# One diffusion layer on one Trainium2 core: the third and fourth part of the first modulation from split float32r operands

## The chip, the cores and the metric

One NeuronCore of a Trainium2 chip runs the whole kernel in one launch. The metric is the device time in microseconds (us), median of several executions; lower is better. Inputs and outputs are float32.

## What is computed

One layer of a latent diffusion backbone: 1024 latent tokens and 256 context tokens of 1024 features, with two SwiGLU feed-forward blocks (inner width 2816) around a mixing block of attention and a short convolution. What matters here is the modulation. A vector `c` (and `c_ctx` for the context tokens) gives nine rows of 1024 numbers, of which rows 0 and 1 shift and scale the input of the first feed-forward block:

```python
m  = (silu(c)     @ w_ada + b_ada).reshape(b, 1, 9, d)
mc = (silu(c_ctx) @ w_ada + b_ada).reshape(1, 1, 9, d)
x   = x   + 0.5 * m[:, :, 2]  * swiglu(rmsnorm(x, g)   * (1 + m[:, :, 1])  + m[:, :, 0],  w_in, w_out)
ctx = ctx + 0.5 * mc[:, :, 2] * swiglu(rmsnorm(ctx, g) * (1 + mc[:, :, 1]) + mc[:, :, 0], w_in, w_out)
```

The mixing block and the second feed-forward block follow in the same manner, and a final RMSNorm.

## The kernel before, in words

Features lie on the 128 partitions, in eight chunks (`KD` = 8, index d or k), tokens along the free dimension. The latent tokens are two blocks of 512, `L0` and `L1`; the context tokens are one block of 256, `CX`. Matrix products with float32 operands are done as three float32r matmuls: an operand is split into a high part (a ScalarE cast to float32r) and a low part (the float32 value less the high part, rounded to float32r), and high times high, high times low and low times high are added in PSUM.

**Modulation rows 0 and 1.** `ada01(e, chs)` computes them in four parts, e = 0 to 3. Part e covers features 256e to 256e + 255 of both rows, which are the norm chunks d = 2e and 2e + 1. Its weights are two tiles of 128 x 4 x 512 floats (1 MB each), loaded by `load_ch`. It is a float32 matmul (L113) with the two columns of `cs` (silu of `c` and of `c_ctx`) as the stationary operand and 512 columns of weights moving, for eight k; each float32 matmul stands in the trace as two passes. ScalarE copies the result to SBUF (`mrow`, L116), PE transposes it in four pieces (`pc`, L121), and DVE adds the bias into `mod` (L124) and forms the scale `amod` (L127).

**Norm chunks.** `norm_chunk(b, which, d)` multiplies x by `amod` and by the reciprocal norm on DVE (L246), adds the shift and casts to the high part on ScalarE (L248), and makes the low part on DVE (L249). For CX the product goes to a temporary `nt`; for L0 and L1 it stays in place.

**The head** (`head`, L760 to L861) is the order around the change. It loads x of L0, the weights of parts 0 and 1 and the first units of the feed-forward weights, forms the L0 norm, and computes parts 0 and 1. Then it loads the weights of part 2 (two tiles of the tag `hh`), x of CX and L1, and the weights of part 3 (in the tile `A2`). The first two feed-forward units of L0 are then done by k: `pf(d)` is a block of twelve matmuls (four units, three products) for chunk d, into four PSUM banks of the tag `in`. Between these blocks stand, in the order of the program:

- after `pf(1)`: the square sum of CX and its norm into the temporary `rcx`, the square sum of L1 (its norm goes into the temporary `rl1`), and `cx_norm` of chunks 0 to 3;
- before `pf(3)`: part e = 2; after it, its `mrow`, transposes and `mod`, the L0 chunks 4 and 5, the rest of the L1 norm, L1 chunks 0 to 3, and CX chunks 4 and 5;
- before `pf(5)`: part e = 3; after it, the same with L0 chunks 6 and 7 and CX chunks 6 and 7;
- then the gated products of L0 (`sg`), the rest of L1's chunks, the two context units (L292 to L294, PSUM tags `o` and `in`), and `conv_by_k` for L1 (L402 to L404), beside which DVE makes the sums and differences of `tsum_steps` (`t1f` and the T tiles). Phase A (L508 to L510) follows.

L1's high and low parts of chunks 4 to 7 share the tile `A2` with the weights of part 3.

**What sets the order.** The program is written in one order; a scheduler that runs while the kernel is built orders each engine's instructions by the order of the program and by when they become ready by its own estimate. Each engine then works through its list in that order. Temporaries come from pools: `t2` is one tag with six buffers of 128 x 512 floats, for the squares `sq` and sums `ssum`, `rcx`, `rl1`, `nt`, `mrow`, `sg`, `t1f`, the sums `s1`, `s2`, `s4` of a unit's weights (L485 to L487) and more. A tile waits until a buffer of its tag is free. In PSUM the tag `in` has four banks, `o` three and `m` one; `pm` and `pc` of `ada01` and the sums of CX use `o`.

```python
def t2(name, shape=None, dt=F32):
    return tp.tile(shape or [P, 512], dt, tag="t2", name=name, bufs=6)
```

In the head all loads are issued by SP. GpSimd (POOL) first appears with `s1`, `s2`, `s4` of unit 2 (L485 to L487, piece "S" of `prep`, called in `head` beside step 5 of `conv_by_k`, behind piece "gA", which casts `wgA`).

Of the kernel before, what the change touches and what calls it, by code (L numbers as in the profile page):

```python
# [6 lines left out]
F32 = mybir.dt.float32  # L7
F32R = mybir.dt.float32r
AF = mybir.ActivationFunctionType
ALU = mybir.AluOpType  # L10
AX = mybir.AxisListType

P = 128
D = 1024
KD = D // P
# [12 lines left out]
def layer_kernel(  # L28
# [18 lines left out]
    pe, act, dve, sp = nc.tensor, nc.scalar, nc.vector, nc.sync  # L47

    base = ctx.enter_context(tc.tile_pool(name="base", bufs=1))
# [3 lines left out]
    def slot(tag, shape, dt, name):  # L53
        return base.tile(shape, dt, tag=tag, name=name)

    def t2(name, shape=None, dt=F32):
        return tp.tile(shape or [P, 512], dt, tag="t2", name=name, bufs=6)
# [4 lines left out]
    cst = base.tile([P, 148], F32, name="cst")  # L62
    sp.dma_start(cst, const_d)
    ident = cst[:, 0:128]
# [12 lines left out]
    cs = base.tile([P, 2, 8], F32, name="cs")  # L77
    mod = base.tile([P, 2, 9, 8], F32, name="mod")
    amod = base.tile([P, 2, 3, 8], F32, name="amod")

    def col(nm, i=0, n=1):
        return vec[:, OFF[nm] + i:OFF[nm] + i + n]
# [7 lines left out]
    def ps(tag, shape, name):  # L90
        return psum.tile(shape, F32, tag=tag, name=name, bufs=psbufs[tag])
# [8 lines left out]
    def finish_mod(j, ms):  # L100
        for m in ms:
# [5 lines left out]
            if m in (2, 8):  # L107
                dve.tensor_scalar(mod[:, j, m, :], mod[:, j, m, :], 0.5, None, op0=ALU.mult)

    def ada01(e, chs):  # L110
        pm = ps(PTAG, [2, 512], "pm01")
        for k in range(KD):
            pe.matmul(pm, cs[:, :, k], chs[k // 4][:, k % 4, :], start=(k == 0), stop=(k == KD - 1))  # L113
        yield
        mrow = t2("mrow", [2, 512])
        act.copy(mrow, pm)  # L116
        yield
        pc = ps("o", [P, 2, 2, 2], "pc")
        for m in range(2):
            for i in range(2):  # L120
                pe.transpose(pc[:, m, i, :], mrow[:, m * 256 + i * P:m * 256 + (i + 1) * P], ident[0:2, 0:2])  # L121
        bias = col("b", 0, 16).rearrange("p (m d) -> p m d", m=2)
        for j in range(2):
            dve.tensor_tensor(mod[:, j, 0:2, 2 * e:2 * e + 2], pc[:, :, :, j], bias[:, :, 2 * e:2 * e + 2], op=ALU.add)  # L124
        for i in range(2):
            d = 2 * e + i
            dve.tensor_scalar(amod[:, :, 0, d], mod[:, :, 1, d], 1.0, col("nf1", d), op0=ALU.add, op1=ALU.mult)  # L127
# [58 lines left out]
    def load_x(b, src, t0):  # L186
        v = src.rearrange("(d p) t -> p d t", p=P)
        for h in range(2):
            sp.dma_start(b.x[h], v[:, 4 * h:4 * h + 4, t0:t0 + b.N])
# [36 lines left out]
    def split_h(b, dt_name):  # L226
        hi = slot(b.htags[0], [P, KD, b.N], F32R, f"h{b.name}h")
        lo = slot(b.htags[1], [P, KD, b.N], F32R, f"h{b.name}l")
        return hi, lo

    def norm_stat_steps(b, r=None, tag="m", e=dve):
        N = b.N
        s = t2("ssum", [P, N])
        act.activation(s, xd(b, 0), AF.Square)
        for d in range(1, KD):
            q = t2("sq", [P, N])
            act.activation(q, xd(b, d), AF.Square)
            e.tensor_tensor(s, s, q, op=ALU.add)
            if d % 2 == 1:
                yield  # L240
        b.r = rstd_bcast(s, N, D, b.name, tag, r)

    def norm_chunk(b, which, d, keep=True):
        hi, lo = b.h
        t = t2("nt", [P, b.N]) if keep else xd(b, d)
        dve.scalar_tensor_tensor(t, xd(b, d), amod[:, b.j, which, d:d + 1], b.r, op0=ALU.mult, op1=ALU.mult)  # L246
        bias = mod[:, b.j, (0, 3, 6)[which], d:d + 1]
        act.activation(hi[:, d, :], t, AF.Identity, bias=bias)  # L248
        dve.scalar_tensor_tensor(lo[:, d, :], t, bias, hi[:, d, :].bitcast(F32), op0=ALU.add, op1=ALU.subtract)  # L249
# [16 lines left out]
    pool = nc.gpsimd  # L266
# [35 lines left out]
    def adv(gen, n=1):  # L302
        for _ in range(n):
            if next(gen, "end") == "end":
                return False
        return True
# [447 lines left out]
    def x_slots(b):  # L754
        b.x = [slot(t, [P, 4, b.N], F32, f"x_{b.name}") for t in b.xtags]

    PTAG = "o"
    F1 = FFN(1, wi1_d, wo1_d, 2, 0, "01c", "A3", "A2")

    def head():  # L760
        L0.h = split_h(L0, "h")
        units = [(ff, n) for ff in range(2) for n in ("g", "u")]
        ch = {}

        def load_ch(e, tags):
            if len(tags) == 1:
                t = slot(tags[0], [P, 2, 4, 512], F32, "ach")
                ch[e] = [t[:, 0], t[:, 1]]
            else:
                ch[e] = [tp.tile([P, 4, 512], F32, tag=t, name="ach", bufs=2) for t in tags]  # L770
            for i in range(2):
                sp.dma_start(ch[e][i].rearrange("p k c -> p (k c)"), ada01_d[2 * e + i])

        load_x(L0, xt_d, 0)
        load_ch(0, ("A2",))
        F1.load_one(*units[0])
        load_ch(1, ("A3",))
        warm = ps("in", [P, 128], "warm")
        for _ in range(30):
            pe.matmul(warm, ident, ident, start=True, stop=True)  # L780
        for _ in norm_stat_steps(L0):
            pass
        for e in range(2):
            a01 = ada01(e, ch[e])
            next(a01)
            if e == 1:
                for d in range(2):
                    norm_chunk(L0, 0, d, False)
                for u in units[1:]:
                    F1.load_one(*u)  # L790
            next(a01)
            next(a01, None)
        load_ch(2, ("hh", "hh"))
        load_x(CX, ctxt_d, 0)
        x_slots(L1)
        load_x(L1, xt_d, 512)
        load_ch(3, ("A2",))
        CX.h = split_h(CX, "h")
        pt = {u: ps("in", [P, 512], "pf") for u in units}
        hi, lo = L0.h  # L800
        for d in range(2, 4):
            norm_chunk(L0, 0, d, False)

        def pf(d):
            for u in units:
                w = F1.w[u[0]][u[1]]
                wh = w[:, 0, d * P:(d + 1) * P]
                wl = w[:, 1, d * P:(d + 1) * P]
                pe.matmul(pt[u], wh, hi[:, d, :], start=(d == 0), stop=False)
                pe.matmul(pt[u], wl, hi[:, d, :], start=False, stop=False)  # L810
                pe.matmul(pt[u], wh, lo[:, d, :], start=False, stop=(d == KD - 1))

        def l1_norm(ds):
            for d in ds:
                norm_chunk(L1, 0, d, False)

        def cx_norm(ds):
            for d in ds:
                norm_chunk(CX, 0, d)

        F1.split_l1()
        for d in range(KD):
            if d in (3, 5):
                e = (d + 1) // 2
                a01 = ada01(e, ch[e])
                next(a01)
            pf(d)
            if d == 1:
                for _ in norm_stat_steps(CX, t2("rcx", [P, 256]), "o"):
                    pass  # L830
                s1 = norm_stat_steps(L1, t2("rl1"))
                adv(s1, 4)
                cx_norm(range(0, 4))
            if d in (3, 5):
                next(a01)
                next(a01, None)
                norm_chunk(L0, 0, 2 * e, False)
                norm_chunk(L0, 0, 2 * e + 1, False)
            if d == 3:
                adv(s1, 9)  # L840
                l1_norm(range(0, 4))
                cx_norm(range(4, 6))
            if d == 5:
                cx_norm(range(6, KD))
        for ff in range(2):
            F1.gated(ff, L0, pt[(ff, "g")], pt[(ff, "u")])
        l1_norm(range(4, 6))
        F1.conv(0, CX, "o")
        l1_norm(range(6, KD))
        F1.conv(1, CX, "in")  # L850
        F1.load(2)
        ts = F1.tsum_steps()
        for i, _ in enumerate(F1.conv_by_k((0, 1), L1)):
            adv(ts)
            if i == 5:
                F1.prep(2, "gA")
                F1.prep(2, "S")
        for piece in ("sA", "sB", "uA"):
            F1.prep(2, piece)
        run(ts)  # L860
        F1.load(3)  # L861

    def run(g):
        for _ in g:
            pass
# [12 lines left out]
    def last_a(F):  # L878
# [6 lines left out]
        return last  # L885

    head()
    F1.phase_b_init()
    F1.phase_a(2, side_a, {2: ("gA",), 3: ("S",), 4: ("sA",), 7: ("uA",), 8: ("sB",)}, last_a(F1))
# [945 lines left out]
```

## Time and profile before

| | |
|---|---|
| runs of the kernel before | 2165.2, 2167.05 and 2167.07 us; median 2167.05 |
| the profiled execution | 2168.2 us, of which its trace spans 2166.4 |
| TensorE (PE) matmuls | 2130.6 us busy, 98% of the span, 10084 instructions |
| PE weight loads (PEld) | 1711.8 us, 79% |
| VectorE (DVE) | 1546.3 us, 71% |
| ScalarE (ACT) | 910.1 us, 42% |
| GpSimd (POOL) | 227.6 us, 11%, 158 instructions |
| granted clock of PE | 0.995 of full speed, as a mean |

The trace is of one execution. A busy time is a sum over instructions; matmuls are pipelined, so a busy PE is not a PE at its peak. The share over the whole span says little of the head, which is the first 108 us; a change there is read from its own stretch. A granted clock of 1.00 is 2.4 GHz, one of 0.50 is 1.2 GHz.

### The profile page before, as it was taken

What the parts mean: (1) busy time and instruction counts of PE and PEld (TensorE: products, weight loads), DVE (VectorE), ACT (ScalarE), POOL (GpSimd) and SP (SyncE); (2) the same over time, 40 slices, a digit from 0 to 9 for tenths busy, and PEclk for the clock granted to TensorE, in tenths of its full rate; (3) what the DMA queues carried; (4) which work ended last, traced back from release to release, by engine and by line L of the source; (5) the groups of instructions that cost most, each with busy time, mean ns of one, the idle gap of its engine ahead of it and who ended that gap; (6) DMA issues with size and microseconds to landing.
All of it is one profiled execution on the core that took longest, in us unless ns stands there. A gap on an engine that the chain in (4) does not pass through costs nothing.

```text
span 2166.4 us, 26536 instructions
## 1 busy us (share of the span) xinstructions
PE 2130.6 (98%) x10084; PEld 1711.8 (79%) x10084; DVE 1546.3 (71%) x2109; ACT 910.1 (42%) x1415; POOL 227.6 (11%) x158
## 2 busy tenths in 40 slices
PE   8999999999999999999999999999999999999998
PEld 4788788888889887887777777777788888877877
DVE  5887776666657867661898899876866666668754
ACT  4422322222335533442567777754422232234433
POOL 0001111101010110000100100001011111123001
PEclk9999999999999999999999999999999999999998
DMA  8043344545379756342211101142232322378642
GB/s 323 16 146 127 124 147 138 167 130 170 127 242 341 263 178 228 119 136 68 88 49 30 40 20 68 49 151 73 78 99 101 117 94 91 107 287 283 225 147 78
DMA packets 111824, 296.01 MB, mean 137 GB/s; under 512 B 10704, under 2 KB 17872, under 8 KB 108624
## 3 DMA queue, kind: packets, MB, share of 16 engines
q1 hardware_dynamic: 111696, 294.32, 40.1%
q8 instruction: 79, 1.29, 0.2%
q14 instruction: 49, 0.40, 0.1%
HBM read 235.29 MB, written 56.36 MB: 135 GB/s over the span
## 4 chain that ended last, share of the span: by engine, by line
PE 75%; DVE 6%; DMA 4%; issue 2%; ACT 2%; POOL 0%; DVEq 0%; SPq 0%; ACTq 0%; POOLq 0%
PE p L508 9%; PE p L510 9%; PE p L509 9%; PE po L704 6%; PE po L706 6%; PE po L705 6%; DMA wa<-in_ada_dram 3%; PE pT L1331 1%; PE pT L1330 1%; PE pmo L1110 1%; PE pmo L1111 1%; PE pmo L1112 1%; PE pvo L1354 1%; PE pvo L1355 1%; PE pvo L1353 1%
## 5 line engine op out<-in xcount | busy, mean ns | idle before, releaser
L704 PE MATMUL po<-gst,wo 128*128 128x512 f32 (+1 forms) x636 | 248.4, 391 | 3.4 <-DVE x L667 3.4
L706 PE MATMUL po<-gst,wo 128*128 128x512 f32 (+1 forms) x636 | 247.2, 389 | 4.0 <-DVE wo L310 4.0
L705 PE MATMUL po<-gst,wo 128*128 128x512 f32 (+1 forms) x636 | 247.3, 389 | 0.0
L309 ACT CAST gst<-grt 128x1024 fp32r<-128x1024 f32 (+1 forms) x95 | 88.9, 936 | 218.7 <-PE po L706 96.4
L310 DVE TENSOR_TENSOR gst<-grt,gst 128x1024 fp32r<-128x1024 f32 (+1 forms) x95 | 110.6, 1165 | 73.7 <-ACT gst L309 73.5
L706 PEld LDWEIGHTS po<-gst,wo 128*128 128x128 f32 x636 | 120.0, 189 | 31.9 <-DVE wo L310 5.1
L704 PEld LDWEIGHTS po<-gst,wo 128*128 128x128 f32 x636 | 120.1, 189 | 31.5 <-issue 2.7
L705 PEld LDWEIGHTS po<-gst,wo 128*128 128x128 f32 x636 | 120.2, 189 | 26.4
L142 DVE SCALAR_TENSOR_TENSOR acc<-wa,cs,acc 128x1024 f32<-128x1024 f32 x70 | 90.5, 1314 | 60.3 <-DMA wa<-in_ada_dram 60.3
L508 PE MATMUL p<-h0h,wgA 128*128 128x512 f32 x320 | 126.6, 396 | 0.2 <-ACT e1f L528 0.2
L509 PE MATMUL p<-h0l,wgA 128*128 128x512 f32 x320 | 126.4, 395 | 0.0
L510 PE MATMUL p<-h0h,wgA 128*128 128x512 f32 x320 | 126.4, 395 | 0.0
L1333 ACT ACTIVATE pexp<-pT 128x512 f32<-128x512 f32 x160 | 94.5, 598 | 66.6 <-PE pT L1331 35.1
L309 ACT CAST wsB<-s 128x512 fp32r<-128x512 f32 x80 | 48.5, 620 | 152.9 <-DVE s L495 83.0
L277 DVE TENSOR_TENSOR wm<-wr,wm 128x1024 fp32r<-128x1024 f32 x52 | 64.8, 1249 | 42.3 <-ACT wm L273 42.0
L310 DVE TENSOR_TENSOR wo<-wr,wo 128x1024 fp32r<-128x1024 f32 x72 | 83.3, 1163 | 15.2 <-ACT wo L309 15.2
L310 DVE TENSOR_TENSOR wsA<-s,wsA 128x512 fp32r<-128x512 f32 x80 | 51.8, 687 | 54.3 <-ACT wsA L309 54.3
L309 ACT CAST wo<-wr 128x1024 fp32r<-128x1024 f32 x72 | 70.3, 976 | 27.2 <-DVE wr L628 16.1
L309 ACT CAST wuA<-wr 128x1024 fp32r<-128x1024 f32 (+1 forms) x40 | 33.5, 838 | 107.6 <-issue 58.7
L309 ACT CAST wsA<-s 128x512 fp32r<-128x512 f32 x80 | 45.6, 618 | 68.9 <-PE p L510 63.1
L508 PEld LDWEIGHTS p<-h0h,wgA 128*128 128x128 f32 x320 | 60.1, 188 | 14.6 <-ACT e1f L528 0.6
L510 PEld LDWEIGHTS p<-h0h,wgA 128*128 128x128 f32 x320 | 60.1, 188 | 14.5
(1077 smaller groups left out, 5966.8 us busy)
## 6 DMA issues: line engine op xcount, KB each, us to landing
wr<-in_wo_dram SPq DMA_DIRECT2D x92, 512.0 KB, 4.7
wr<-in_wi_dram SPq DMA_DIRECT2D x88, 512.0 KB, 3.7
wa<-in_ada_dram SPq DMA_DIRECT2D x56, 512.0 KB, 3.6
wr<-in_wmi_dram SPq DMA_DIRECT2D x38, 512.0 KB, 3.6
grt<-g1P SPq DMA_DIRECT2D x35, 512.0 KB, 4.8
grt<-g2P SPq DMA_DIRECT2D x35, 512.0 KB, 6.0
g1P<-ev SPq DMA_DIRECT2D x35, 256.0 KB, 3.2
g2P<-ev SPq DMA_DIRECT2D x35, 256.0 KB, 2.0
```

Of the source, the lines that this page charges most:

```text
L142: dve.scalar_tensor_tensor(acc[:, i, :], w, cs[:, j, k:k + 1], acc[:, i, :], op0=ALU.mult, op1=ALU.add)
L277: dve.tensor_tensor(w[:, 1, :], r, w[:, 0, :].bitcast(F32), op=ALU.subtract)
L309: act.copy(hi, t)
L310: dve.tensor_tensor(lo, t, hi.bitcast(F32), op=ALU.subtract)
L508: pe.matmul(pt, w[:, 0, c:c + P], hi, start=(k == 0 and not more), stop=False, skip_group_check=more)
L509: pe.matmul(pt, w[:, 0, c:c + P], lo, start=False, stop=False, skip_group_check=more)
L510: pe.matmul(pt, w[:, 1, c:c + P], hi, start=False, stop=(k == 3), skip_group_check=more)
L704: pe.matmul(o, wh, hi, start=st, stop=False, skip_group_check=g)
L705: pe.matmul(o, wh, lo, start=False, stop=False, skip_group_check=g)
L706: pe.matmul(o, wl, hi, start=False, stop=end, skip_group_check=g)
L1110: pe.matmul(pt, wh, hi[:, k, :], start=(i == 0), stop=False)
L1333: act.activation(p, pt, AF.Exp)
```

## The change

For the parts e = 2 and e = 3 the float32 matmul with two columns is replaced. A new tile `csr` holds the split of `cs`: in its first half the high parts of both columns and, as columns 3 and 4, their low parts; in its second half the high parts again and zeros. It is made once by `cs_split`, called in `head` after the second `load_ch` and before the L0 norm. For each k the weights are split into `hi` (ScalarE cast, tile `chi`) and `lo` (POOL subtraction, tile `clo`), both `t2` tiles, and two float32r matmuls with four columns are accumulated into `pm`, which has four rows. The copy `mrow` and the transposes take four rows instead of two, and two more additions on DVE put the rows of low parts onto `mod`. Parts 0 and 1 stay as they were.

```diff
--- before.py
+++ after.py
@@ -107,21 +107,44 @@
             if m in (2, 8):
                 dve.tensor_scalar(mod[:, j, m, :], mod[:, j, m, :], 0.5, None, op0=ALU.mult)
 
+    csr = base.tile([P, 2, 8, 4], F32R, name="csr")
+
+    def cs_split():
+        csv = cs.rearrange("p a b -> p b a")
+        zero = cst[:, 0:16].rearrange("p (b a) -> p b a", a=2)
+        act.copy(csr[:, 0, :, 0:2], csv)
+        act.copy(csr[:, 1, :, 0:2], csv)
+        act.activation(csr[:, 1, :, 2:4], zero, AF.Identity, scale=0.0)
+        dve.tensor_tensor(csr[:, 0, :, 2:4], csv, csr[:, 0, :, 0:2].bitcast(F32), op=ALU.subtract)
+
     def ada01(e, chs):
-        pm = ps(PTAG, [2, 512], "pm01")
+        n = 2 if e < 2 else 4
+        pm = ps(PTAG, [n, 512], "pm01")
         for k in range(KD):
-            pe.matmul(pm, cs[:, :, k], chs[k // 4][:, k % 4, :], start=(k == 0), stop=(k == KD - 1))
+            w = chs[k // 4][:, k % 4, :]
+            if e < 2:
+                pe.matmul(pm, cs[:, :, k], w, start=(k == 0), stop=(k == KD - 1))
+            else:
+                hi = t2("chi", dt=F32R)
+                lo = t2("clo", dt=F32R)
+                act.copy(hi, w)
+                pool.tensor_tensor(lo, w, hi.bitcast(F32), op=ALU.subtract)
+                pe.matmul(pm, csr[:, 0, k, :], hi, start=(k == 0), stop=False)
+                pe.matmul(pm, csr[:, 1, k, :], lo, start=False, stop=(k == KD - 1))
         yield
-        mrow = t2("mrow", [2, 512])
+        mrow = t2("mrow", [n, 512])
         act.copy(mrow, pm)
         yield
-        pc = ps("o", [P, 2, 2, 2], "pc")
+        pc = ps("o", [P, 2, 2, n], "pc")
         for m in range(2):
             for i in range(2):
-                pe.transpose(pc[:, m, i, :], mrow[:, m * 256 + i * P:m * 256 + (i + 1) * P], ident[0:2, 0:2])
+                pe.transpose(pc[:, m, i, :], mrow[:, m * 256 + i * P:m * 256 + (i + 1) * P], ident[0:n, 0:n])
         bias = col("b", 0, 16).rearrange("p (m d) -> p m d", m=2)
         for j in range(2):
-            dve.tensor_tensor(mod[:, j, 0:2, 2 * e:2 * e + 2], pc[:, :, :, j], bias[:, :, 2 * e:2 * e + 2], op=ALU.add)
+            mv = mod[:, j, 0:2, 2 * e:2 * e + 2]
+            dve.tensor_tensor(mv, pc[:, :, :, j], bias[:, :, 2 * e:2 * e + 2], op=ALU.add)
+            if n == 4:
+                dve.tensor_tensor(mv, mv, pc[:, :, :, 2 + j], op=ALU.add)
         for i in range(2):
             d = 2 * e + i
             dve.tensor_scalar(amod[:, :, 0, d], mod[:, :, 1, d], 1.0, col("nf1", d), op0=ALU.add, op1=ALU.mult)
@@ -775,6 +798,7 @@
         load_ch(0, ("A2",))
         F1.load_one(*units[0])
         load_ch(1, ("A3",))
+        cs_split()
         warm = ps("in", [P, 128], "warm")
         for _ in range(30):
             pe.matmul(warm, ident, ident, start=True, stop=True)
```

## Rows read from the trace of the kernel before

**Rows 1.** Busy us (PE, PEld, DVE, ACT, POOL) by stretch, clock, DMA share, GB/s

```profile
54.00:56.00 2.00, 2.00 (x4) 0.39 (x3) 2.00 (x5) 2.00 (x4) 0.00 (x0) 0.50 0.01 4
...
75.00:80.00 5.00, 5.00 (x31) 4.40 (x30) 3.42 (x6) 3.76 (x6) 0.00 (x0) 1.00 0.07 29
...
95.00:100.00 5.00, 5.00 (x23) 4.00 (x23) 5.00 (x9) 3.71 (x8) 0.00 (x0) 1.00 0.00 0
```

**Rows 2.** Timeline, 41 to 73 us: start, us, engine, line, operation, tiles, count

```profile
43.09 7.03 PE L113 MATMUL pm<-ach,cs 128*2 128x512 f32 x16
...
51.83 0.56 ACT L116 COPY mrow<-pm 2x512 f32<-2x512 f32 x1
...
52.51 0.40 PE L121 MATMUL pc<-cst,mrow 2*128 2x2 f32 x4
...
53.31 5.29 PE L113 MATMUL pm<-ach,cs 128*2 128x512 f32 x8
...
54.14 1.41 DVE L246 SCALAR_TENSOR_TENSOR x<-x,amod,rbs 128x512 f32<-128x512 f32 x2
...
61.53 3.60 PE L113 MATMUL pm<-ach,cs 128*2 128x512 f32 x8
...
65.21 0.58 ACT L116 COPY mrow<-pm 2x512 f32<-2x512 f32 x1 [3.20 <-PE pm L113]
...
70.16 1.41 DVE L246 SCALAR_TENSOR_TENSOR x<-x,amod,rbs 128x512 f32<-128x512 f32 x2
...
72.39 0.40 PE L809 MATMUL pf<-h0h,wg 128*128 128x512 f32 x1
```

**Rows 3.** Timelines (ACT, POOL, DVE), 53 to 91 us: `t2` users and `wgA`

```profile
53.95 1.05 ACT L309 CAST wgA<-wr 128x1024 fp32r<-128x1024 f32 x1
...
82.31 1.30 POOL L485 TENSOR_TENSOR s<-wr 128x512 f32<-128x512 f32 x1 [81.87 <-DMA g1c<-sg]
...
90.09 0.68 DVE L427 TENSOR_TENSOR t1f<-x,x 128x512 f32<-128x512 f32 x1
```

**Rows 4.** Waits of POOL, whole span: total us, times, longest (one of them)

```profile
POOL s L485 <- DMA g2b<-sg: 94.1, 1, 94.1
```

**Rows 5.** Timeline, 50 to 67 us: what gives `t2` buffers back

```profile
50.44 0.88 DVE L249 SCALAR_TENSOR_TENSOR hcl<-nt,mod,hch 128x256 fp32r<-128x256 f32 x2
...
50.58 1.05 PE L196 MATMUL ss<-cst,ssum 128*128 128x1 f32 x8 [0.46 <-DVE ssum L238]
...
53.09 0.87 DVE L249 SCALAR_TENSOR_TENSOR hcl<-nt,mod,hch 128x256 fp32r<-128x256 f32 x2
...
66.23 0.48 DVE L249 SCALAR_TENSOR_TENSOR hcl<-nt,mod,hch 128x256 fp32r<-128x256 f32 x1 [1.54 <-ACT hch L248]
```

**Rows 6.** Groups by line (first two: to 120 us): busy us, mean ns

```profile
L309 ACT CAST T<-t1f 128x512 fp32r<-128x512 f32 x4 | 2.4, 619 | 6.6 <-DVE t1f L427 6.6
...
L124 DVE TENSOR_TENSOR mod<-pc,vec 128x4 f32<-128x4 f32 x8 | 0.9, 157 | 5.2 <-PE pc L121 5.2
...
L583 POOL TENSOR_TENSOR gt<-ev 128x512 f32<-128x512 f32 x10 | 16.3, 1635 | 30.5 <-issue 17.1 <-DVE ev L579 8.0 <-DMA wr<-in_wi_dram 5.4
...
L585 POOL TENSOR_TENSOR gt<-e1f,ev 128x512 f32<-128x512 f32 x10 | 14.2, 1418 | 209.5 <-DVE ev L579 209.5
```

**Rows 7.** Timelines, 208 to 215 us: an accumulation without and with POOL beside it

```profile
208.19 1.28 DVE L142 SCALAR_TENSOR_TENSOR acc<-wa,cs,acc 128x1024 f32<-128x1024 f32 x1
...
211.05 2.28 DVE L142 SCALAR_TENSOR_TENSOR acc<-wa,cs,acc 128x1024 f32<-128x1024 f32 x1
...
212.33 2.15 POOL L554 TENSOR_TENSOR ev<-e1f,ev 128x512 f32<-128x512 f32 x1
```

**Rows 8.** SP's issues of e=2's weights (start, us), and a DMA's us to landing

```profile
21.57 0.91 SPq L772 DMA_DIRECT2D ach<-in_ada_dram  x2
...
ach<-in_ada_dram SPq DMA_DIRECT2D x1, 1024.0 KB, 9.1
```

## The prediction

> **What bounds it now.** I read first how busy the engines are stretch by stretch [rows 1], then the order of time from 41 to 73 us [rows 2]. TensorE (PE) is the bound of nearly the whole kernel: from 72.39 us, where the sixth block of `pf` begins, to the first product of phase A it has no idle slice (5.00 of 5.00 us from 75 to 80 and from 95 to 100) [rows 1]. So whatever sets the start of that block sets the end of the kernel, if what follows is unchanged. Ahead of it stands one chain, walked twice: the sixteen PE passes of a modulation part, ScalarE's copy `mrow`, four transposes, DVE's small additions, and then the first norm chunk that uses the new scale. Part e=2 has its passes at 43.09 (7.03 us), `mrow` at 51.83, the chunk at 54.14. Part e=3 has its passes in two groups of eight (53.31 and 61.53), `mrow` at 65.21, the chunk at 70.16, the block of `pf` at 72.39 [rows 2].
>
> The second thing to read is who gets a `t2` buffer, for the change takes 32 of them and the pool has six. Buffers seem to be handed out in the order of the program, not of readiness. The cast `wgA` of the next unit is pulled forward to 53.95, while the sum `s1`, the next piece in the program, whose input comes with the same loads, runs at 82.31 after GpSimd (POOL) has idled 81.87 us, released by the store of a context `sg` [rows 3]. Counting back from `s1` in the program gives `t1f` four times and the two context `sg`: six tiles, so `s1` has to wait for the first `sg` to be stored, which is what the row says; and a `t1f` ahead of it is written only at 90.09, after `s1` [rows 3]. The second FFN shows the same wait, 94.1 us [rows 4].
>
> **Removed.** For e=2 and e=3 the float32 matmuls: 16 passes in 7.03 us, 0.44 us each [rows 2]. In their place 16 float32r matmuls of the same 512 columns; a stream of such runs 23 in 5.00 us, 0.22 each [rows 1], so 3.5 us. PE is relieved of 3.5 us for each part, and of more where the second part ran at a granted clock of 0.50, 1.2 GHz (54 to 56 us) [rows 1], after PE had waited.
>
> **Added.** Once: three small ScalarE copies and a DVE subtraction, before x has landed, when both engines wait for it; I cost them at nothing, at worst some 0.2 us each if x were early. For each part: eight casts 128x512 on ScalarE at 0.62 us, eight subtractions on POOL, and two DVE additions at 0.16 us [rows 6]. POOL's subtraction of this size lies between 1.30 [rows 3] and 2.15 us [rows 7]; groups of ten average 1.42 and 1.64 [rows 6]; I take 1.5. No DMA is added, and none is queued behind the new waits on SP. On POOL nothing waits behind the subtractions before `s1`. On ScalarE the casts stand in one queue with the norm chunks, so a cast without a buffer can hold those up.
>
> What the rows show of POOL beside DVE: a DVE operation with two inputs in SBUF takes 2.28 us instead of 1.28 while POOL runs, and POOL's 2.15 in the same place [rows 7]. The Trainium skill (SBUF — State Buffer, section on the two separate sides) says the shared port pair is an exclusive lock held for the whole instruction, against a DVE operation with two SBUF inputs as well. These rows agree. By that rule alone the eight subtractions (8 x 1.30) and DVE's L1 chunks of the same time (some 7 us) would stand end to end, and the result would be about 2188 us; by the mean of the rows it is the sum below.
>
> **When e=2's split can run.** `rcx` and `rl1` hold two of the six buffers throughout. The other four go, in program order, through L1's squares, the four context tiles `nt`, and only then to `chi` and `clo`. So the first `chi` has a buffer when the second `hcl` is written, 50.44 + 0.88 = 51.32; `clo` when the L1 sum has gone through PE, 51.63; the second pair when the third and fourth `hcl` are written, the last at 53.09 + 0.87 = 53.96 [rows 5]. It does not help that the weights landed by about 31 us [rows 8]. Cast to 51.94, first low part to 53.4, second from 53.96 to 55.46, six more at 1.5 (two pairs in flight keep POOL going) to 64.5, the last matmul to 64.7. From `mrow` to the chunk it was 2.31 us [rows 2], now 0.31 more: chunk at 67.3 instead of 54.14, 13.2 us later. PE's place at 43.09 stays empty.
>
> **e=3.** After the last pair the four buffers go to `mrow`, two `nt` and one `chi`. `clo` needs the buffer of `mrow`, free after the transposes, 1.08 us after `mrow` starts [rows 2]: 65.8. Low part to 67.3, matmuls to 67.7. While the two `nt` are held, one pair runs at a time: 0.62 + 1.5 + 0.44 = 2.56 us. Both are free after the last `hcl`, which ended 12.6 us after the chunk (66.71 [rows 5] against 54.14); about 5.6 of these were eight L1 chunk operations (0.70 each by the pair at 54.14), now done while DVE waits. That gives 74.3. Two more pairs go singly to 72.8, the last five at 1.5 to 80.3, the last matmul to 80.5, and 2.62 to the chunk: 83.1 instead of 70.16, 13 us later. In this time PE has only `pf` blocks four and five and the first context products, so it cannot use the wait; POOL, ScalarE's casts and the buffers set the pace, and PE's saved 7 us lie beside them.
>
> **Sum.** From that chunk on PE's work is what it was, so the whole 13 us reach the end. The profiled execution took 2168.2 us, 1.15 above the median of 2167.05: 2168.2 + 13 - 1.15 = 2180.
>
> **Bounds.** POOL at 1.30 and the `nt` buffers back at once: e=2 ends at 63.3, its transposes at 64.4, e=3's eight low parts at 74.8, chunk at 77.6, +7.5 us, so 2174.5. POOL at 2.15 throughout: e=2's chunk at 71.8; e=3's first pair at 72.9, two single ones at 3.2, five at 2.15 to 90, chunk at 92.9, +22.7 us, so 2190. A granted clock of 0.50 during the sparse matmuls makes each 0.44; that is mostly beside POOL and is worth 1 or 2 us within these bounds.
>
> **Rivals.**
> (1) *Faster.* Buffers are given to whoever is ready. Then POOL begins when the weights are in, near 31 us [rows 8], has e=2's eight low parts done at about 43.6 under `pf` blocks one to three, and e=3's by about 56. PE then takes 3.5 instead of 7.03 us for e=2 and 3.5 instead of 5.29 + 3.60 for e=3 [rows 2], up to 8.9 us; but DVE is full from 54 to 56 and 95 to 100 us [rows 1] and loses time to POOL, so I pass on 6.5: 2160.5. It decides if the first low part stands before 45 us. Against it stand the waits of [rows 3, 4], with POOL idle and the data there. Chance 0.11.
> (2) *No change.* The wait is there but PE finds other work: context and L1 products pulled forward. They need PSUM of the tag `o` behind both parts' `pm` and `pc`, or the four `in` banks that `pf` holds until its end, so at most a few us of them can move. It would come to 2167, with 4 us either way. Chance 0.08.
> (3) *Not what it says.* A float32r matmul with four columns could take a full float32 pass. Then PE has 7.03 us as now, still beside POOL's 12: the forecast stays, and (1) becomes no change. It has no chance of its own.
>
> **Numbers.** Slower for the reason above has 0.81. About 0.2% (4.3 us) is what a measurement of this kernel can tell from no change. The range of the likeliest case alone is 2174.5 to 2190; with some 3 us below for (2) and 1 above for the clock it is 2171 to 2191, leaving out (1), half of (2) and a tail. Faster 0.11, same 0.08, slower 0.81.
>
> **What would show it.** Right: the first low part on POOL after 51 us and the last of e=3 near 80; eight of them per part, 1.3 to 2.2 us each; PE nearly idle from 43 to 50.6 and thinly used to 67, at a granted clock of 0.50 in parts; e=2's chunk near 67, e=3's near 83, phase A 13 us later, the rest shifted. The step on `nt` is wrong if e=3's low parts come without gaps. The forecast fails if low parts run before 45 us, or if PE is full between 45 and 65.

## The result, and the profile after

The changed kernel is slower: median 2191.11 us (2186.3 to 2196.2, four runs) against 2166.12 us for the kernel before on the same chip, a ratio of 1.0116 with a 95% interval of 1.0102 to 1.0130. The forecast was 2180 with a range of 2171 to 2191. The direction came as written, and so did the mechanism for part e=2; the step for e=3 did not. The kernel lost 25.0 us where 13 were forecast, and the median lies just above the range. The profiled execution took 2191.7 us (before: 2168.2).

| | before | after |
|---|---|---|
| PE busy us, instructions | 2130.6, 10084 | 2132.9, 10084 |
| DVE | 1546.3, 2109 | 1550.3, 2114 |
| ACT | 910.1, 1415 | 920.0, 1434 |
| POOL | 227.6, 158 | 252.3, 174 |
| granted clock | 0.995 | 0.988 |

The number of matmuls is the same (32 passes became 32 matmuls) and PE is busy as long as before, though each matmul should take half: the table does not show where the time went. The head does. First PE's timeline after the change, from 42 us on; the bracket is the idle time before the instruction and what released it.

```profile
42.64 0.43 PE L234 MATMUL rb<-cst,rs 128*128 128x128 f32 x2 [0.55 <-DVE rs L227]
50.87 1.87 PE L219 MATMUL ss<-cst,ssum 128*128 128x1 f32 x8 [7.80 <-DVE ssum L261]
...
54.96 0.59 PE L133 MATMUL pm<-clo,csr 128*4 128x512 f32 x1 [0.75 <-POOL clo L131]
...
66.18 0.58 PE L141 MATMUL pc<-cst,mrow 4*128 4x4 f32 x4 [0.67 <-ACT mrow L136]
70.35 0.80 PE L833 MATMUL pf<-h0h,wg 128*128 128x512 f32 x1 [3.59 <-ACT h0h L271]
...
89.07 0.58 PE L141 MATMUL pc<-cst,mrow 4*128 4x4 f32 x4 [0.67 <-ACT mrow L136]
...
94.91 0.40 PE L833 MATMUL pf<-h0h,wg 128*128 128x512 f32 x1
```

The first two rows show what e=2's sixteen passes had been worth [rows 2]: their place is empty, 7.80 us of it, because the next work, the L1 sums `ss`, waits for DVE's `ssum` to 50.87, and in the kernel before the same sums started at 50.58 [rows 5]. Those passes had filled a hole; taking them out saves nothing. The third row is one of fifteen in which a matmul waits for POOL's low part (7.5 us in all), the fifth a wait of 3.59 us for ScalarE. The last row is the sixth block of `pf`, 22.5 us later than in [rows 2]. That is nearly all of the 23.5 us between the two profiled executions.

Next the clock and the busy time of PE, PEld, DVE, ACT and POOL by stretch of the changed kernel.

```profile
46.00:50.00 4.00, 0.00 (x0) 0.00 (x0) 3.30 (x7) 2.26 (x5) 0.00 (x0) 0.54 0.10 40
50.00:54.00 4.00, 2.56 (x10) 2.04 (x10) 2.59 (x8) 1.73 (x5) 0.37 (x1) 0.50 0.01 2
54.00:60.00 6.00, 4.70 (x12) 1.12 (x11) 4.37 (x3) 4.43 (x8) 5.91 (x5) 0.50 0.00 0
60.00:66.00 6.00, 3.67 (x8) 0.35 (x7) 0.05 (x1) 1.33 (x3) 4.87 (x4) 0.50 0.00 0
...
84.00:90.00 6.00, 4.57 (x13) 1.27 (x14) 1.03 (x4) 3.08 (x5) 3.76 (x4) 0.50 0.00 0
90.00:94.00 4.00, 4.00 (x20) 4.00 (x20) 4.00 (x12) 1.78 (x3) 0.00 (x0) 0.50 0.00 0
95.00:100.00 5.00, 5.00 (x23) 4.05 (x22) 3.07 (x6) 3.12 (x4) 0.00 (x0) 1.00 0.00 0
```

After PE's empty stretch the granted clock is 0.50, and it is so again from 84 to 94 us, behind e=3's sparse matmuls. That is one reason why PE's busy sum did not fall: at 0.50 a float32r matmul of 512 columns takes 0.59 to 0.63 us, against 0.39 in the last row's stretch. The other is that these matmuls stand apart, while in that stretch the next one begins 0.23 us after the last, so that their times overlap. In all, the 32 matmuls keep PE busy for 15.4 us, and the 32 passes did for 15.9. From 60 to 66 us DVE is idle (0.05 us busy) and ScalarE mostly so, and PE's matmuls wait again and again for POOL's next low part: POOL sets the pace.

Now POOL, then the rows of ScalarE and DVE between which the rest of the time lies.

```profile
53.63 11.25 POOL L131 TENSOR_TENSOR clo<-ach,chi 128x512 fp32r<-128x512 f32 x8 [53.19 <-ACT chi L130]
75.92 11.84 POOL L131 TENSOR_TENSOR clo<-ach,chi 128x512 fp32r<-128x512 f32 x8 [11.05 <-ACT chi L130]
105.54 1.28 POOL L508 TENSOR_TENSOR s<-wr 128x512 f32<-128x512 f32 x1 [17.78 <-DVE t1f L450]
```

```profile
52.78 0.26 ACT L225 ACTIVATE sd<-ss,small 128x4 f32<-128x4 f32 x1 [2.02 <-PE ss L219]
52.94 0.61 ACT L130 CAST chi<-ach 128x512 fp32r<-128x512 f32 x1
...
65.55 0.57 ACT L136 COPY mrow<-pm 4x512 f32<-4x512 f32 x1 [3.08 <-PE pm L133]
66.03 0.57 ACT L237 COPY rl<-rb 128x512 f32<-128x512 f32 x1
67.92 1.45 ACT L271 ACTIVATE b<-x,mod 128x512 fp32r<-128x512 f32 x2 [1.32 <-DVE x L269]
69.58 1.38 ACT L271 ACTIVATE h0h<-x,mod 128x512 fp32r<-128x512 f32 x2 [0.21 <-DVE x L269]
73.55 1.38 ACT L271 ACTIVATE b<-x,mod 128x512 fp32r<-128x512 f32 x2 [2.59 <-DVE x L269]
74.84 0.49 ACT L271 ACTIVATE hch<-nt,mod 128x256 fp32r<-128x256 f32 x1
75.24 0.61 ACT L130 CAST chi<-ach 128x512 fp32r<-128x512 f32 x1
```

```profile
66.80 0.16 DVE L145 TENSOR_TENSOR mod<-pc,vec 128x4 f32<-128x4 f32 x1 [6.75 <-PE pc L141]
...
68.80 1.41 DVE L269 SCALAR_TENSOR_TENSOR x<-x,amod,rbs 128x512 f32<-128x512 f32 x2
...
91.14 1.41 DVE L269 SCALAR_TENSOR_TENSOR x<-x,amod,rbs 128x512 f32<-128x512 f32 x2
```

POOL's sum `s1` [rows 3] comes 23.2 us later, the shift of everything behind the head, and no longer waits for a stored context but for DVE's `t1f`. Read with [rows 2]: e=2's chunk moved from 54.14 to 68.80, 14.7 us; e=3's from 70.16 to 91.14, 21.0 us. The second figure is the one to explain. `rl`, the copy of L1's scale, stood at 53.47 in the kernel before:

```profile
53.47 0.58 ACT L214 COPY rl<-rb 128x512 f32<-128x512 f32 x1 [0.27 <-PE rb L211]
```

Now it stands behind e=2's eight casts and behind `mrow`, at 66.03. So the chunks of L1, which need it, were not done while DVE waited 6.75 us, but afterwards; and ScalarE's casts for them (`b`), together with those of e=2's own chunk (`h0h`, `hch`), stand ahead of e=3's first cast at 75.24. Between `mrow` and that cast ScalarE is not the slow engine: it waits for DVE and holds its list while it does.

### The profile page after: what moved, and what is told of

It reads as the page before. It is cut to its first block, busy times and chain, and to the rows that moved or that the text cites. A ratio compares the mean times of both kernels' runs of the same rounds, so it can differ in the third digit from the quotient of the medians.

```text
span 2189.9 us, 26599 instructions
## 1 busy us (share of the span) xinstructions
PE 2132.9 (97%) x10084; PEld 1714.0 (78%) x10084; DVE 1550.3 (71%) x2114; ACT 920.0 (42%) x1434; POOL 252.3 (12%) x174
## 4 chain that ended last, share of the span: by engine, by line
PE 77%; DVE 8%; DMA 5%; issue 3%; ACT 2%; POOL 0%; SPq 0%; DVEq 0%; ACTq 0%; POOLq 0%
PE p L533 10%; PE p L531 10%; PE p L532 10%; PE po L727 5%; PE po L729 5%; PE po L728 5%; DMA wa<-in_ada_dram 3%; DVE acc L165 2%; PE pT L1355 1%; PE pT L1354 1%; PE pmo L1134 1%; PE pmo L1135 1%; PE pmo L1136 1%; PE pc L590 1%; PE pc L591 1%
## 5 line engine op out<-in xcount | busy, mean ns | idle before, releaser
L533 PEld LDWEIGHTS p<-h0h,wgA 128*128 128x128 f32 x320 | 60.1, 188 | 14.5
L531 PEld LDWEIGHTS p<-h0h,wgA 128*128 128x128 f32 x320 | 60.1, 188 | 14.5 <-ACT e1f L551 0.5
```

Of the source, the lines that this page charges most:

```text
L531: pe.matmul(pt, w[:, 0, c:c + P], hi, start=(k == 0 and not more), stop=False, skip_group_check=more)
L533: pe.matmul(pt, w[:, 1, c:c + P], hi, start=False, stop=(k == 3), skip_group_check=more)
```

## The experiments

All are edits of the changed kernel, and times are medians beside runs of the kernel before on the same chip (2167.3 to 2167.9 us).

**The queue: L1's scale ahead of e=2's casts.**

```diff
-                adv(s1, 4)
+                adv(s1, 9)
```

> Edit: five more steps of L1's norm are issued before part e=2, so that the copy of L1's scale (rl) stands ahead of e=2's eight casts in ScalarE's list. Theory (e=3 lost its time because L1's chunks, and the ScalarE casts they feed, stood between e=2's casts and e=3's first one): rl runs near 54 us instead of 66, the L1 chunks run on DVE from 55 to 67 us while it waited before, e=3's first cast comes at 66 to 68 us instead of 75.24, e=3's chunk near 83 instead of 91.14, and the kernel takes 2182 to 2185 us. Rival (buffers and GpSimd alone set e=3, ScalarE's order does nothing): e=3's first cast within 1 us of 75 and 2189 to 2193 us. A second rival: the L1 chunks beside GpSimd's subtractions slow both, e=2's eight low parts then take over 2 us each and the gain of e=3 is given back: 2188 us or more with e=2's chunk past 72 us.

Measured: 2192.51 us, ratio 1.0111 (1.0096 to 1.0126). `rl` did run at 53.64, and the L1 chunks did move into e=2's stretch. POOL of this kernel, and its windows from 56 to 72 us:

```profile
56.01 3.14 POOL L131 TENSOR_TENSOR clo<-ach,chi 128x512 fp32r<-128x512 f32 x2 [55.57 <-DVE hcl L272]
59.58 1.65 POOL L131 TENSOR_TENSOR clo<-ach,chi 128x512 fp32r<-128x512 f32 x1 [0.43 <-DVE hcl L272]
...
67.14 4.77 POOL L131 TENSOR_TENSOR clo<-ach,chi 128x512 fp32r<-128x512 f32 x3 [2.55 <-ACT chi L130]
77.91 1.51 POOL L131 TENSOR_TENSOR clo<-ach,chi 128x512 fp32r<-128x512 f32 x1 [6.01 <-ACT chi L130]
```

```profile
56.00:72.00 16.00, 7.89 (x16) 1.09 (x16) 12.72 (x11) 8.00 (x13) 12.27 (x8) 0.50 0.00 0
```

The theory fell in this form, and the second rival held on the chunk and the time, though not on over 2 us for each low part (1.53 as a mean for e=2): e=2's low parts now run from 56.0 to 71.9 us with POOL busy for 12.27 and DVE for 12.72 of the 16 us, its chunk comes at 74.75, e=3's at 94.02. POOL's gaps end with DVE's `hcl` and ScalarE's `chi`; the subtractions themselves are only sometimes longer (1.31 us as the median of sixteen, at most 2.07), so it is more the lists than the subtraction's length. One part of the theory held: from `mrow` to e=3's first cast it is now 4.7 us (72.58 to 77.23) instead of 9.7 (65.55 to 75.24). But `mrow` itself comes 7 us later, so the interleaved L1 work is as much in the way of e=2 as it was of e=3, and in this order the L1 chunks cannot be had for nothing beside POOL's subtractions.

**The other way round: e=3's casts ahead of e=2's chunks.** Part e=3 is begun as soon as e=2's scale is out.

```diff
-            if d in (3, 5):
-                e = (d + 1) // 2
-                a01 = ada01(e, ch[e])
+            if d == 3:
+                a01 = ada01(2, ch[2])
                 next(a01)
...
                 next(a01)
                 next(a01, None)
+                if d == 3:
+                    a01 = ada01(3, ch[3])
+                    next(a01)
                 norm_chunk(L0, 0, 2 * e, False)
```

> Edit: part e=3 is begun as soon as e=2's scale is out, ahead of e=2's chunks in the program; buffers and engines stay. Theory (the step that failed is the place of e=3's first cast on ScalarE): that cast comes at 65 to 68 us instead of 75.24, the eight low parts end by 80, e=3's chunk comes at 80 to 84 us instead of 91.14, and the kernel takes 2180 to 2185 us. Rival (what is moved out of the way comes back: L1's chunks and the context, now behind e=3's casts, hold PE afterwards): e=3's chunk as early as that, but 2188 us or more.

Measured: 2185.58 us, 1.0083 (1.0064 to 1.0102), about 6 us better than the changed kernel. Rows of ScalarE, POOL and DVE:

```profile
65.91 1.65 ACT L130 CAST chi<-ach 128x512 fp32r<-128x512 f32 x3
```

```profile
66.60 5.42 POOL L131 TENSOR_TENSOR clo<-ach,chi 128x512 fp32r<-128x512 f32 x4 [1.85 <-ACT chi L130]
...
73.97 4.37 POOL L131 TENSOR_TENSOR clo<-ach,chi 128x512 fp32r<-128x512 f32 x3 [0.26 <-POOL clo L131]
```

```profile
69.04 3.53 DVE L269 SCALAR_TENSOR_TENSOR x<-x,amod,rbs 128x512 f32<-128x512 f32 x2
...
86.90 1.41 DVE L269 SCALAR_TENSOR_TENSOR x<-x,amod,rbs 128x512 f32<-128x512 f32 x2
```

The cast stands at 65.91 and the low parts end at 78.3, as the theory had it, so the place on ScalarE's list held e=3's split back by 9 us. (The edit also puts e=3's claims on the shared buffers ahead of those of two `nt`. But in the changed kernel ScalarE was not waiting before the cast at 75.24; it was at the work that stands ahead of it.) Of these 9 us, 4 reach e=3's chunk (86.90 against 91.14, where the theory wanted 80 to 84): the transposes now stand behind `pf` products (82.44) and the chunk behind the L1 chunks, and e=2's two chunk operations take 3.53 us beside POOL instead of 1.41. The time is half a microsecond above the theory's upper end.

**One part at a time.** In the next two kernels only e=3, and only e=2, is split.

```diff
-        n = 2 if e < 2 else 4
+        n = 2 if e < 3 else 4
...
-            if e < 2:
+            if n == 2:
```

> Edit: only part e=3 is split, e=2 runs as in the kernel before. Theory (each part loses by its own start: e=2 by buffers, 14.7 us, e=3 by ScalarE's list, 6.3 us more): e=2's chunk is back near 54 us; e=3's first cast waits for mrow and the L1 chunks' casts and stands at 57 to 62 us, its eight low parts take 12 us, its chunk comes at 73 to 78 us instead of 70.16 before, and the kernel takes 2169 to 2174 us. Rival (the loss belongs to e=3, whose part e=2's delay merely overlaps): e=3's chunk past 84 us and 2181 us or more. A second rival (e=3's split fits into the wait and PE's saved 3.5 to 5 us count): 2161 to 2165 us.

Measured: 2176.54 us, 1.0040 (1.0027 to 1.0052). e=2's chunk is back at 54.21, e=3's first cast stands at 61.99 as the theory had it, but its chunk comes at 78.86, 0.9 us past the theory's end, and the time is 2.5 us past it. POOL's group names what it waited for last: the L1 chunks (`b`), not the weights.

```profile
62.67 12.80 POOL L131 TENSOR_TENSOR clo<-ach,chi 128x512 fp32r<-128x512 f32 x8 [62.23 <-DVE b L272]
```

```diff
-        n = 2 if e < 2 else 4
+        n = 4 if e == 2 else 2
...
-            if e < 2:
+            if n == 2:
```

> Edit: only part e=2 is split, e=3 runs in float32 as in the kernel before. Theory (the two losses add: e=3 alone cost 9.3 us, both 24): e=2's chunk at 67 to 70 us, e=3's some 12 to 16 us later as in the kernel before, and the kernel takes 2178 to 2184 us. Rival (PE uses e=2's wait for e=3's sixteen passes, so e=2's delay is half hidden): e=3's chunk within 8 us of e=2's, 2172 to 2177 us.

Measured: 2179.92 us, 1.0057 (1.0037 to 1.0076), 12.4 us over the kernel before. e=2's chunk is at 68.44 and e=3's at 81.96, both as the theory had them, and so is the time. Part e=2 alone costs what the forecast gave for the whole change (13 us). With the 8.6 us of e=3 alone it makes 21.0, against 25.0 for both together. The intervals of the three (about 4, 3 and 3 us either way) are too wide to say that the difference of 4 us is more than chance, and by the start of the sixth `pf` block the two make 21.9 us against 22.5 (table below). So the two losses add, as the theory had it.

**The price of the low parts.** First they are left out altogether: one matmul for each k, the low parts of these weights missing from the product.

```diff
                 hi = t2("chi", dt=F32R)
-                lo = t2("clo", dt=F32R)
                 act.copy(hi, w)
-                pool.tensor_tensor(lo, w, hi.bitcast(F32), op=ALU.subtract)
-                pe.matmul(pm, csr[:, 0, k, :], hi, start=(k == 0), stop=False)
-                pe.matmul(pm, csr[:, 1, k, :], lo, start=False, stop=(k == KD - 1))
+                pe.matmul(pm, csr[:, 0, k, :], hi, start=(k == 0), stop=(k == KD - 1))
```

> Edit: no low part; each k is one float32r matmul of the cast weights, so the low parts of these weights are left out of the product. The shared buffers and the order stay. Theory (the program order of the shared buffers sets the start): the first cast still stands at 50 to 53 us though no subtraction exists, e=2's chunk comes at 60 to 62 us (8 casts of 0.62 us and the chain to the chunk) instead of 54.14 before, e=3's first cast again waits for what stands ahead of it on ScalarE, and the kernel takes 2172 to 2180 us. Rival (the subtractions are the loss): 2160 to 2168 us.

Measured: 2177.20 us, 1.0043 (1.0027 to 1.0059). ScalarE's casts:

```profile
53.05 0.61 ACT L129 CAST chi<-ach 128x512 fp32r<-128x512 f32 x1
54.37 3.72 ACT L129 CAST chi<-ach 128x512 fp32r<-128x512 f32 x7
...
68.53 0.60 ACT L129 CAST chi<-ach 128x512 fp32r<-128x512 f32 x1
```

With no subtraction and half the matmuls the split still begins at 53.05 and e=3's part at 68.53, e=2's chunk comes at 62.74, and the kernel is still 9.9 us slower than before. That is the theory, though the first chunk is 0.7 us past its end. So about 10 of the 25 us are the place and the length of the casts, and 15 the low parts, with their matmuls and the buffers they take. Then the same low parts by DVE, in the same buffers:

```diff
-                pool.tensor_tensor(lo, w, hi.bitcast(F32), op=ALU.subtract)
+                dve.tensor_tensor(lo, w, hi.bitcast(F32), op=ALU.subtract)
```

> Edit: the sixteen low parts are made by DVE instead of GpSimd; buffers and order stay. Theory (buffers set the start, GpSimd's 1.45 us each only the length): e=2's first low part still stands past 51 us, the eight take 0.7 to 1 us each, e=2's chunk comes 3 to 5 us earlier than 68.80, e=3's by 6 to 10 us earlier than 91.14, and the kernel takes 2181 to 2186 us. Rival A (GpSimd's rate is the whole loss): 2166 to 2172 us. Rival B (DVE's own list is the next queue: the subtractions stand behind, and in front of, L1's chunks): no gain, 2188 to 2196 us.

Measured: 2180.18 us, 1.0058 (1.0043 to 1.0073), 11 us better than the change and as the theory had it: first low part at 53.34, 0.69 us each, e=2's chunk at 63.88, e=3's at 82.19; the time is 0.8 us under the theory's lower end.

**Buffers of their own.** The pairs no longer come from `t2`, but from two pairs in one further weight tile.

```diff
+        if e == 2:
+            ring[0] = wp.tile([P, 2, 1024], F32R, tag="wu", name="cw", bufs=5)
...
-                hi = t2("chi", dt=F32R)
-                lo = t2("clo", dt=F32R)
+                hi = ring[0][:, k % 2, 0:512]
+                lo = ring[0][:, k % 2, 512:1024]
```

> Edit: high and low parts come from two pairs of buffers of their own instead of the six shared t2 buffers; the split and its engines are the same. Theory (the shared buffers, handed out in program order, hold the split back until 51 us): the first two low parts run before 40 us, e=2's matmuls start near 43 to 45 us and end by 55 us (GpSimd at 1.45 each), e=2's chunk comes near 57 us instead of 68.80, e=3's near 72 to 75 instead of 91.14, and the kernel takes 2167 to 2172 us. Rival (GpSimd's rate, or its sharing with DVE, sets the loss wherever the buffers are): the low parts start early but take over 2 us each, or e=2's chunk stays past 64 us, and the kernel takes 2182 us or more.

Measured: 2180.02 us, 1.0053 (1.0038 to 1.0068). The theory missed: a gain of about 11 us over the changed kernel, 8 short of what it wanted. The rival held on the chunk (65.67, past 64) and was 2 us too high in the time. POOL, PE and DVE:

```profile
34.66 3.06 POOL L135 TENSOR_TENSOR cw<-ach,cw 128x512 fp32r<-128x512 f32 x2 [34.22 <-ACT cw L134]
45.96 2.95 POOL L135 TENSOR_TENSOR cw<-ach,cw 128x512 fp32r<-128x512 f32 x2 [8.25 <-ACT cw L134]
...
61.25 4.47 POOL L135 TENSOR_TENSOR cw<-ach,cw 128x512 fp32r<-128x512 f32 x3 [2.76 <-ACT cw L134]
```

```profile
42.63 0.47 PE L136 MATMUL pm<-cw,csr 128*4 128x512 f32 x1
```

```profile
60.93 0.74 DVE L273 SCALAR_TENSOR_TENSOR x<-x,amod,rl 128x512 f32<-128x512 f32 x1
...
63.27 2.48 DVE L154 TENSOR_SCALAR amod<-mod,vec 128x2 f32<-128x2 f32 x2
65.67 1.40 DVE L273 SCALAR_TENSOR_TENSOR x<-x,amod,rbs 128x512 f32<-128x512 f32 x2
```

The first low part stands at 34.66 instead of 53.63: the shared buffers had indeed held the split back. Then the next holds appear one by one. The third low part waits 8.25 us. Both pairs are full until PE takes the first, at 42.63, behind its `pf` blocks; then ScalarE casts, but only between the squares of L1. And while POOL runs, DVE's two tiny `amod` operations of 128x2 take 2.48 us instead of 0.35. That is 2.1 us of the 8.7 by which e=2's chunk, at 65.67, is later than the 57 expected. The Trainium skill (SBUF — State Buffer, section on the two separate sides) says that GpSimd and a VectorE operation that has two SBUF inputs or runs in a two-port mode exclude each other on a shared port pair for a whole instruction. The times agree with such a lock, for the two `amod` take 1.24 and 1.32 us and the shortest subtraction 1.27; whether `amod`, with one tensor as input, runs in a two-port mode, no run here shows.

**Buffers of their own, and an earlier place.** Part e=2 is begun before `pf(1)` (the lines below show this edit alone); in the second kernel e=3 is also begun right behind e=2's chunks; in the third the low parts are DVE's besides.

```diff
-            if d in (3, 5):
-                e = (d + 1) // 2
+            if d in (1, 5):
+                e = (d + 3) // 4 + 1
```

> Edit: two pairs of buffers of their own, and part e=2 is begun four pf blocks' worth earlier in the program, ahead of the context's sum of squares. Theory (the loss is where the split stands, not that it is made): e=2's low parts run from 33 to 47 us beside the pf blocks, its chunk comes at 54 to 58 us, e=3's low parts from about 50 to 66, e=3's chunk at 69 to 74 us, and the kernel takes 2164 to 2170 us. Rival (GpSimd and DVE hold each other up wherever the split stands): with the L0 chunks and sums in that stretch e=2's chunk stays past 62 us, e=3's past 78, and the kernel takes 2175 us or more.

> Edit: as the last, and part e=3 is begun right behind e=2's chunks instead of two pf blocks later. Theory: e=3's low parts run from about 48 to 60 us, its chunk comes at 62 to 68 us instead of 70.16 before, the sixth pf block starts before 72 us, and the kernel takes 2158 to 2166 us, under the kernel before. Rival (the waits only move): PE's first blocks or the L1 and context chunks, now behind e=3's casts, come later by as much, and the kernel takes 2168 to 2176 us.

> Edit: as the last, with the low parts made by DVE. Theory (GpSimd's 1.45 us each is the pace of the split once buffers and place are right): eight low parts take 6 to 7 us, e=2's matmuls are done by 42 us, e=3's chunk comes at 56 to 62 us, and the kernel takes 2155 to 2163 us, 2 to 5 us under the last. Rival (DVE is the fuller engine there): DVE's sums and chunks come 5 us or more later, and the kernel takes as long as the last or longer.

Measured: 2180.50 us (1.0061, 1.0044 to 1.0078), 2176.09 (1.0042, 1.0027 to 1.0057) and 2175.48 (1.0033, 1.0020 to 1.0046). All three theories missed. The rivals' times held: the second to 0.1 us, and the third in so far as 0.6 us under the second kernel cannot be told from no gain. But the first rival gave another reason than the rows show. Rows of POOL and ScalarE of the first kernel:

```profile
35.22 10.68 POOL L135 TENSOR_TENSOR cw<-ach,cw 128x512 fp32r<-128x512 f32 x8 [34.78 <-ACT cw L134]
```

```profile
39.54 0.62 ACT L134 CAST cw<-ach 128x512 fp32r<-128x512 f32 x1 [0.61 <-POOL cw L135]
...
42.54 0.41 ACT L261 ACTIVATE ssum<-x_c 128x256 f32<-128x256 f32 x1
...
50.59 0.37 ACT L241 COPY rcx<-rb 128x256 f32<-128x256 f32 x1 [0.78 <-PE rb L238]
```

The eight low parts run without a gap under the `pf` blocks, as wanted. But each of ScalarE's casts waits for POOL to give its buffer back, and the squares of the context stand behind them: they begin at 42.54, and `rcx` comes at 50.59 where the changed kernel has 43.11. The whole chain of norms behind it, L1's with it, is 7.5 us late, and e=2's chunk comes at 64.28. In the other two `rcx` stands at 50.02 and 47.05. Started early, the split delays the norms; started late, it delays the chunk.

**Only the part that is on PE's path, with buffers of its own.** In the kernel before PE is busy throughout from 54 to 66 us (12.0 of 12), around e=3's two groups of passes [rows 2], so this is where removing them could pay. (Not all of it: where only e=3 was split, PE waited 2.32 us for `h0h` before 55.77, so the first group had filled a hole as well.)

```diff
-        n = 2 if e < 2 else 4
+        n = 2 if e < 3 else 4
+        if e == 3:
+            ring[0] = wp.tile([P, 2, 1024], F32R, tag="wu", name="cw", bufs=5)
...
```

> Edit: only part e=3 is split, with two pairs of buffers of its own. Theory (e=3 is the part in which PE has no idle time, so its passes are worth removing if the split is early enough): the first low part comes at 50 to 53 us, the last by 66, e=3's chunk at 67 to 70 us against 70.16 before, and the kernel takes 2161 to 2167 us. Rival (ScalarE and DVE are the chain there, and the casts and GpSimd's sharing with DVE lengthen it): e=2's chunk past 56 us, e=3's past 72, and 2169 to 2176 us.

> Edit: as the last, with the low parts made by DVE. Theory (GpSimd's pace is what is left): low parts 0.7 us each, the last by 62 us, e=3's chunk at 64 to 68 us, and the kernel takes 2159 to 2165 us. Rival (DVE's chunks of the same stretch wait behind the subtractions): as the last or up to 4 us above it.

Measured: 2175.30 us (1.0035, 1.0022 to 1.0049) and 2172.60 (1.0019, 1.0006 to 1.0032). The first low part stands at 50.19 as forecast, and then POOL waits 4.31 us for PE, whose list holds the matmuls among other work:

```profile
50.19 3.00 POOL L135 TENSOR_TENSOR cw<-ach,cw 128x512 fp32r<-128x512 f32 x2 [49.75 <-ACT cw L134]
57.50 6.74 POOL L135 TENSOR_TENSOR cw<-ach,cw 128x512 fp32r<-128x512 f32 x4 [4.31 <-PE pm L136]
```

The rival held for the first (e=2's chunk 56.62, e=3's 75.77); DVE in POOL's place gave 2.7 us (e=3's chunk 72.52), less than the theory and more than the rival had. It is the best of the twelve, at the edge of what can be told from no change, and still not under the kernel before.

**All of them together.** The start of the sixth `pf` block against the change of the median:

| kernel | sixth `pf` block, us later | median, us over before |
|---|---|---|
| the change | 22.5 | 25.0 |
| L1's scale first | 23.4 | 24.6 |
| e=3 first | 16.7 | 18.1 |
| own buffers, e=2 early | 13.1 | 13.2 |
| e=2 alone | 11.8 | 12.4 |
| low parts by DVE | 11.5 | 12.3 |
| own buffers | 10.6 | 12.1 |
| own buffers, both early | 10.4 | 8.8 |
| e=3 alone | 10.1 | 8.6 |
| own buffers, both early, DVE | 8.1 | 8.2 |
| own buffers, e=3 alone | 7.0 | 7.8 |
| no low parts | 6.9 | 9.9 |
| own buffers, e=3 alone, DVE | 3.4 | 5.1 |

The first column is one execution, the second a median, and they agree within 3 us over the whole span of 20. So what is lost up to this block is lost for good: within those 3 us, nothing behind it gives time back.

## Where the prediction was right, and the step that failed

**What bounds it now** held: the start of the sixth block sets the end (table above). **Removed** was right in what it left out of the sum: PE's seven microseconds at 43.09 stayed empty. Its 3.5 us of relief for each part did not come: the sparse matmuls kept PE busy as long as the passes had. **Added**: 1.5 us for a subtraction measured 1.41 and 1.48 (11.25 and 11.84 us for eight). The split of `cs`, taken at nothing, cost nothing: the next context sums stand at 41.59, before at 41.67.

**When e=2's split can run** held but for its start: first low part at 53.63, not 51.94, because ScalarE's first cast (52.94) stands behind `sd`, and that waited for `ss`, which took 1.87 us at a clock of 0.50 instead of 1.05 [rows 5]. The low parts ended at 64.88, only 0.4 us late, and the chunk came at 68.80 against 67.3; between them lie the last matmul at the lower clock and two L1 chunk operations that DVE did ahead of `amod` (67.14 and 67.87). That the buffers keep the split from starting at 34 us is shown by the kernel with buffers of its own.

**e=3** is the step that failed, in one clause: that the eight L1 operations are "now done while DVE waits", so that the first low part could follow the transposes at 65.8. It came at 75.92, 10.1 us later. Against that, the low parts ran without gaps (11.84 us instead of 14.5 with some pairs one at a time behind `nt`, so this part of the step was wrong too, in the other direction), and from the last of them to the chunk it was 3.4 us rather than 2.8. 10.1 - 2.7 + 0.6 is the 8.0 us between 91.14 and the forecast 83.1. The cause is the order on ScalarE's list, where I had followed the buffers alone: with e=3's casts moved ahead, the first low part stands at 66.60. Its worth is another matter. Only about 4 us come back so at e=3's chunk and about 6 at the sixth block and in the median, and the opposite cure brings nothing, since the L1 work then runs against POOL; no order tried saved more with the shared buffers and POOL. In the sum the clause amounts to this: the forecast let e=3's split cost nothing on top of e=2's delay (13.2 us at e=2's chunk, 13 at e=3's), and split alone it costs 8.6 us.

**Sum**: 13 us at e=3's chunk were to reach the end as 13; 21.0 became 22.5 at the sixth block, because the context products ahead of it ran at a clock of 0.50 (89.58 to 94.0), and 25.0 in the medians (23.5 between the two profiled executions). The bounds took the clock at 1 or 2 us, which was about right; they erred by holding the first low part of e=3 fixed.

**Rivals.** *Faster* failed by its own mark, a first low part before 45 us, and the runs that met this mark were slower too: it had left out that ScalarE's and DVE's lists carry the norms on which PE waits in the same stretch. *No change* failed as well: PE was idle, not served with other work. *Not what it says*: at a clock of 1.00 the four-column matmuls take 0.39 us, as the other float32r ones do, so they are of the cheap kind. The 2188 us worked out beside the rule of the Trainium skill (SBUF — State Buffer, section on the two separate sides) come near the measured time by accident: the prediction does not show how its terms make that sum, and in the changed kernel the L1 chunks hardly ran beside POOL at all.

## What to carry to other kernels

Before a matmul is made cheaper, look at what PE does next: passes that fill a wait for another engine can be had for nothing, and removing them buys only a hole and a lower clock. When the price is paid in small operations on other engines, write down each engine's list, in order, with what stands ahead of and behind them; buffers tell when an instruction may start, but the list tells whom it holds up. And if moving the added work about only moves the loss, as in several of these kernels, the work itself does not fit the stretch.

## What the hardware showed beyond expectation

- A DVE operation beside POOL's subtraction can be stretched even if it is tiny: two of 128x2 took 2.48 us instead of 0.35, a chunk operation pair 3.53 instead of 1.41. Not every one is. In the changed kernel DVE's `nt` at 76.22 and `x` at 76.61 took their usual 0.47 and 0.74 us, and the subtraction beside them, from 75.92, took 2.56 us, the longest of the sixteen (shortest 1.27, median 1.28).
- The granted clock of PE fell while PE was idle for 7.8 us (0.54 from 46 to 50 us) and stayed at 0.50 from 50 to 72 us, although PE was busy for 13 of these 22 us. It went back to 1.00 in the dense `pf` blocks, from 74 us on, and fell to 0.50 again at 84 us, among e=3's sparse matmuls. So work removed from PE came back as longer work: from 41.5 us to the sixth block PE was busy for 32.1 us against 29.2 before, and in the whole kernel for 2132.9 against 2130.6.
